# Whole-tile weight splits with three buffers a part, and woven weights prepared two pieces ahead

## The chip, the core and the metric

The program runs on one core of one Trainium2 chip. The metric is the device time of the whole program in microseconds. Three runs of the kernel before took 2589.87, 2593.4 and 2594.01 us; the median is 2593.4 us. The profile and the trace are of one further execution of the same kernel.

## The reference, cut to what matters

Two token groups (512 latent tokens and 128 context tokens, 640 columns in all) go through two layers. Everything is float32.

```python
def trunk_layer(x, cond, ...):
    mod = silu(cond) @ w_ada + b_ada            # six vectors of 1024 each
    h = rmsnorm(x) * (1 + scale1) + shift1
    q, k, v, z, a, b, u_ssm, u_pool, gates = split(h @ w_in)   # 1024 -> 6160 columns
    o_dn   = deltanet(q, k, v, z, a, b)         # chunked, two directions, 4 heads of 128
    o_ssm  = s5(u_ssm)                          # complex diagonal scan, two directions, then GLU
    o_pool = pool_mixer(u_pool)                 # windows 2, 4, 8, 16
    merged = g_dn * (o_dn @ w_branch_dn) + g_ssm * (o_ssm @ w_branch_ssm) \
           + g_pool * (o_pool @ w_branch_pool)
    x = x + gate1 * (merged @ w_out)
    h = rmsnorm(x) * (1 + scale2) + shift2
    return x + gate2 * (ffn(h))                 # 1024 -> 2 x 2816, conv3, silu gate, 2816 -> 1024
```

A final RMSNorm follows, and the last context states of both scans are outputs too.

## The kernel before, in words

**Products in three parts.** A float32 weight tile of 128 output columns arrives in SBUF as `wraw`, 128 partitions by 8 rows of 128 (1024 columns, 512 KB). `wsplit` (L362) makes two fp32r parts of it: `whi`, a rounded copy on ScalarE (called through the wrapper, so the trace gives it as L235 with output `whi`), and `wlo = wraw - whi` on VectorE (L372). `mm3` (L377) then runs, for each of the 8 rows, two matmuls of 320 columns with whi and the high part of the activations (L384), two with whi and the low part (L386) and two with wlo (L388): 48 matmuls a tile, in one double PSUM tile `acc`. In the trace these three lines are nearly all of TensorE's time.

**Buffers of the weights.** `wraw` has `WRAW` = 4 slots of 512 KB. The slots are shared by three users: the weight tiles, the tiles `wada` of w_ada (512 KB each; the adaLN vectors need two per k row, consumed by TensorE at L446 straight from the slot), and one small tile. A slot is given out in turn, so the n-th user waits for the release of the (n-4)-th. A weight tile's slot is released by its wlo; a wada slot by its matmuls. `whi` and `wlo` have `WB` = 4 buffers of `WK` = 4 rows each, so a tile takes two buffers of each part and is split by two ScalarE and two VectorE operations of 512 columns. All loads of weights are issued by SyncE (L359, L443), which also issues the other transfers of the layer and works them off in program order: a transfer that waits for its slot holds up the ones behind it.

**Weaving.** A layer has three long chains with little TensorE work: the S5 state-space stage (`s5_chain`: input products, `s5_in`, the scan on VectorE, `s5_out`), the DeltaNet stage, and the turn between layers. While such a chain is written out, `Weave.run` adds to a credit and emits pieces of other work from a queue `wv`: tiles of the input projection (z, pool, q, k, v, gates), branch products and the adaLN pieces. `Weave.step` emits one piece; where the piece that is next in the queue has weights, its weights are loaded and split ahead of it (`self.w`). What is left in the queue at a stage's end is drained without a chain beside it. The order of the instructions on each engine is then chosen by a list scheduler over the whole program; the code order and the buffers decide what it may choose from.

**S5 output.** For each of 8 groups `qd`, `s5_kernel` (L954) makes a table with matmuls at L964, finishes a small tile on VectorE (L970, L971), stores it to DRAM (L974) and reads it back in eight transfers (L979) as the Toeplitz tile `M`; `s5_out` (L982) multiplies the scanned states by the table (L997, L998) and the inputs by `M` (L999).

**FFN.** The FFN of layer 0 carries two adaLN groups of layer 1: after each weight tile comes one k row with two wada tiles. The FFN has no weave; its tiles are loaded and split one or two ahead by its own loop.

The names of rows in the trace: `whi`, `wlo`, `wraw`, `wada` as above; `pg` a page of the activation arena (its sizes are `PAGES`), `acc` and `sm` PSUM tiles, `hall_dram` and `s_hall` the small S5 tile.

Of the kernel before, what the change touches and what calls it, by code (L numbers as in the profile page):

```python
# [12 lines left out]
F32R = mybir.dt.float32r  # L13
AF = mybir.ActivationFunctionType
OP = mybir.AluOpType
AX = mybir.AxisListType

P = 128
D = 1024
KT = 8  # L20
# [14 lines left out]
NSLOT = 82  # L35
UNIT = 4
PAGE = 2592 // UNIT
PAGES = [5888] + [2592] * 2 + [2560] * 4 + [1280] * 11 + [2592]
EPS = 1e-6
WRAW = 4  # L40
WK, WB = 4, 4
OFF_Q, OFF_K, OFF_V, OFF_Z, OFF_AB = 0, 512, 1024, 1536, 2048
OFF_SSM, OFF_POOL, OFF_G = 2064, 2576, 3088
POOL_WINDOWS = (2, 4, 8, 16)
# [144 lines left out]
class Weave:  # L189
# [3 lines left out]
    def __init__(self, arena):  # L193
        self.arena = arena
        self.q = deque()
        self.credit, self.scale = 0.0, 1.0
        self.w = None

    def add(self, cost, fn, weights=None):

# [8 lines left out]
    def step(self):  # L209
        cost, fn, weights = self.q.popleft()  # L210
        self.arena.side = True
        w = [self.w or weights()] if weights else []
        self.w = self.q[0][2]() if self.q and self.q[0][2] else None
        fn(*w)
        self.arena.side = False
        self.credit -= cost
# [43 lines left out]
def hybrid_dit_kernel(ctx: ExitStack, tc: tile.TileContext, a, outs, depth=DEPTH, taps=None):  # L260
    nc = tc.nc
    V, S, GP, PE = nc.vector, ScalarE(nc.scalar), nc.gpsimd, nc.tensor

    cpool = ctx.enter_context(tc.tile_pool(name="cpool", bufs=1))
    wpool = ctx.enter_context(tc.tile_pool(name="wpool", bufs=1))
# [30 lines left out]

    ar = Arena(ctx.enter_context(tc.tile_pool(name="apool", bufs=1)), PAGES)

# [57 lines left out]
    def wraw(src, c0, nk, ncols):  # L356

        t = wpool.tile([P, nk, ncols], F32, name="wraw", tag="wraw", bufs=WRAW, padded_shape=[P, 8, P])
        nc.sync.dma_start(t, src.rearrange("(k p) m -> p k m", p=P)[:, :, c0:c0 + ncols])  # L359
        return t  # L360

    def wsplit(raw, m):  # L362

        his, los = [], []
        for k in range(0, raw.shape[1], WK):
            ks = slice(k, min(k + WK, raw.shape[1]))
            n = ks.stop - k
            hi = wpool.tile([P, n, P], F32R, name="whi", tag="whi", bufs=WB, padded_shape=[P, WK, P])
            lo = wpool.tile([P, n, P], F32R, name="wlo", tag="wlo", bufs=WB, padded_shape=[P, WK, P])
            src = raw[:, ks, m * P:(m + 1) * P]  # L370
            S.activation(hi, src, AF.Copy)
            V.tensor_sub(lo, src, hi)  # L372
            his.append(hi)
            los.append(lo)
        return Blocks(his), Blocks(los)

    def mm3(ps, w, hs, first=True, last=True, M=P):  # L377

        hi, lo = w
        n = hi.n  # L380
        for k in range(n):
            hh, hl = hs[k]
            for h in range(2):
                PE.matmul(ps[:M, h, :HF], hi[:, k, :M], hh[:, h * HF:(h + 1) * HF], start=first and k == 0, stop=False)  # L384
            for h in range(2):
                PE.matmul(ps[:M, h, :HF], hi[:, k, :M], hl[:, h * HF:(h + 1) * HF], start=False, stop=False)  # L386
            for h in range(2):
                PE.matmul(ps[:M, h, :HF], lo[:, k, :M], hh[:, h * HF:(h + 1) * HF], start=False,  # L388
                          stop=last and k == n - 1)
# [32 lines left out]
    class Stream:  # L422


        def __init__(self, src, c0, ncols, nk=KT):
            self.src, self.c0, self.nk = src, c0, nk

        def tile(self, m):
            return wsplit(wraw(self.src, self.c0 + m * P, self.nk, P), 0)


    def ada_pieces(l, p, mod, grp, E=None):
# [3 lines left out]
        def rows_k(k):  # L436
# [3 lines left out]
            for hf in range(2):  # L440
                t = E() if E else wpool.tile([P, 1024], F32, name="wada", tag="wraw", bufs=WRAW)
                c0 = grp * 2048 + hf * 1024
# [1699 lines left out]
```

## Time and profile before

| | before |
|---|---|
| runs shown | 2589.87, 2593.4, 2594.01 us |
| profiled execution, device time | 2591.93 us |
| its span in the trace | 2590.2 us |
| mean granted TensorE clock | 0.973 of full |
| TensorE matmul busy | 2440.7 us, 94% |
| VectorE busy | 1608.3 us, 62% |
| ScalarE busy | 989.8 us, 38% |
| GpSimd busy | 555.2 us, 21% |
| splits on ScalarE (whi) | 538 instructions, 331.7 us |
| splits on VectorE (wlo) | 538 instructions, 414.5 us |

The span is the time between the first and the last instruction of the profiled execution; the 1.7 us between it and the device time lie around it. The granted clock is the share of TensorE's full speed that the chip gave; 0.5 in a stretch is the lower of its two levels (1.2 and 2.4 GHz). Matmul records in the trace are pipelined, so a stretch where TensorE is busy all the time is read by how many matmuls it holds.

### The profile page before, as it was taken

How to read it: one execution, taken by the hardware profiler on the slowest of the kernel's cores; microseconds unless marked ns; L12 is line 12 of the kernel's file. 1: busy time of each engine (PE TensorE's matmuls, PEld its weight loads, DVE VectorE, ACT ScalarE, POOL GpSimd, SP SyncE). 2: the span in 40 equal slices, each digit the busy share in tenths (PEclk: the TensorE clock that was granted, in tenths of full speed). 3: DMA queues.
4: the chain of work that ended last, by engine and by line, in shares of the span. 5: the costliest groups of instructions: out<-in, count | busy, mean ns of one | idle time of the engine just before them, and what ended most of it. 6: DMA issues, size and time to landing. Idle time of an engine off the chain costs nothing. (4 is left out here: it accounts for less than half of the span.)

```text
span 2590.2 us, 43654 instructions
## 1 busy us (share of the span) xinstructions
PE 2440.7 (94%) x17225; PEld 2321.6 (90%) x17225; DVE 1608.3 (62%) x3250; ACT 989.8 (38%) x1792; POOL 555.2 (21%) x560
## 2 busy tenths in 40 slices
PE   7899989998889999999988999899989999999999
PEld 6688987997789988999988998799879899999998
DVE  5768863269866743553596687633897766445355
ACT  4242342363333531442443423424533354334243
POOL 3521320135342100000134404311445320000000
PEclk8899999999889999999999999999999999999999
DMA  9833327344253255322237232463454322222221
GB/s 309 162 112 94 91 64 233 114 127 140 94 178 95 74 172 178 98 67 81 75 115 103 59 113 79 118 197 99 138 166 160 112 66 74 74 74 78 78 66 66
DMA packets 382016, 297.29 MB, mean 115 GB/s; under 512 B 33706, under 2 KB 336500, under 8 KB 381812
## 3 DMA queue, kind: packets, MB, share of 16 engines
q1 hardware_dynamic: 377892, 286.53, 38.4%
q0 software_dynamic: 3552, 7.73, 1.2%
q8 instruction: 136, 2.23, 0.4%
q14 instruction: 68, 0.56, 0.1%
q10 hardware_dynamic: 368, 0.25, 0.0%
HBM read 251.45 MB, written 42.48 MB: 113 GB/s over the span
## 5 line engine op out<-in xcount | busy, mean ns | idle before, releaser
L384 PE MATMUL acc<-pg,whi 128*128 128x320 f32 x4064 | 943.2, 313 | 5.9 <-ACT pg L235 2.9
L388 PE MATMUL acc<-pg,wlo 128*128 128x320 f32 x4064 | 936.0, 311 | 8.0 <-DVE wlo L372 8.0
L386 PE MATMUL acc<-pg,whi 128*128 128x320 f32 x4064 | 938.0, 311 | 4.9 <-DVE pg L411 4.9
L372 DVE TENSOR_TENSOR wlo<-wraw,whi 128x512 fp32r<-128x512 f32 (+1 forms) x538 | 414.5, 776 | 524.3 <-ACT whi L235 518.1
L384 PEld LDWEIGHTS acc<-pg,whi 128*128 128x128 f32 x4064 | 681.4, 189 | 47.1 <-issue 16.7
L388 PEld LDWEIGHTS acc<-pg,wlo 128*128 128x128 f32 x4064 | 684.5, 189 | 10.5 <-DVE wlo L372 8.9
L386 PEld LDWEIGHTS acc<-pg,whi 128*128 128x128 f32 x4064 | 685.4, 189 | 6.0 <-DVE pg L411 5.4
L235 ACT ACTIVATE whi<-wraw 128x512 fp32r<-128x512 f32 (+1 forms) x538 | 331.7, 623 | 925.4 <-PE acc L386 723.0
L235 ACT ACTIVATE pg<-pg 128x640 f32<-128x640 f32 (+8 forms) x335 | 222.0, 682 | 262.5 <-DVE pg L1996 56.1
L235 ACT ACTIVATE pg<-sm 128x512 f32<-128x512 f32 (+9 forms) x245 | 109.5, 470 | 207.1 <-PE sm L1502 59.4
L235 ACT ACTIVATE pg<-acc 128x640 f32<-128x640 f32 (+3 forms) x196 | 127.0, 655 | 73.9 <-PE acc L388 49.5
L700 DVE SCALAR_TENSOR_TENSOR pg<-pg,cols_f 128x511 f32<-128x511 f32 (+1 forms) x130 | 65.9, 548 | 49.8 <-ACT pg L235 49.7
L411 DVE TENSOR_TENSOR pg<-pg,pg 128x640 fp32r<-128x640 f32 x84 | 68.6, 821 | 41.4 <-ACT pg L235 37.6
L713 POOL DMA_DIRECT2D pg<-in_ssm_lambda_re_dram x2 | 1.2, 583 | 407.9 <-ACT whi L235 407.9
L1685 POOL TENSOR_TENSOR pg<-pg,pg 128x640 f32<-128x640 f32 x21 | 38.9, 1855 | 226.1 <-DVE pg L1683 146.9
L691 DVE SCALAR_TENSOR_TENSOR pg<-acc,mod,pg 128x320 f32<-128x320 f32 x56 | 30.8, 549 | 78.3 <-PE acc L388 78.2
L235 ACT ACTIVATE pg<-acc,cols_f 128x640 f32<-128x640 f32 (+1 forms) x88 | 68.3, 776 | 0.0
L701 DVE SCALAR_TENSOR_TENSOR pg<-pg,cols_h 128x511 f32<-128x511 f32 (+1 forms) x130 | 65.6, 546 | 0.0
L446 PE MATMUL sm<-wada,silu_c 128*32 128x512 f32 x320 | 57.9, 627 | 8.0 <-DMA wada<-in_w_ada_dram 8.0
L1683 DVE SCALAR_TENSOR_TENSOR pg<-pg,acc 128x640 f32<-128x640 f32 x48 | 39.0, 817 | 40.9 <-PE acc L388 35.3
L906 POOL TENSOR_TENSOR pg<-pg,pg 128x512 f32<-128x512 f32 (+1 forms) x32 | 54.7, 1710 | 1.9
L901 POOL TENSOR_TENSOR pg<-s_cp,pg 128x640 f32<-128x640 f32 x16 | 27.6, 1725 | 127.4 <-PE acc L388 55.8
(392 smaller groups left out, 2960.8 us busy)
## 6 DMA issues: line engine op xcount, KB each, us to landing
wraw<-in_w_in_dram SPq DMA_DIRECT2D x96, 512.0 KB, 4.4
wraw<-in_ffn_w_up_dram SPq DMA_DIRECT2D x88, 512.0 KB, 3.9
wada<-in_w_ada_dram SPq DMA_DIRECT2D x80, 512.0 KB, 4.4
wraw<-in_ffn_w_down_dram SPq DMA_DIRECT2D x32, 512.0 KB, 3.9
mg_dram<-pg SPq DMA_DIRECT2D x32, 320.0 KB, 2.2
pg<-mg_dram SPq DMA_DIRECT2D x32, 320.0 KB, 5.2
wraw<-in_w_out_dram SPq DMA_DIRECT2D x16, 512.0 KB, 3.9
pg<-in_w_ada_dram SPq DMA_DIRECT2D x6, 1024.0 KB, 10.8
```

The costliest lines, as they stand in the source:

```text
L235: ins = self.engine.activation(out, in_, func, **kw)
L372: V.tensor_sub(lo, src, hi)
L384: PE.matmul(ps[:M, h, :HF], hi[:, k, :M], hh[:, h * HF:(h + 1) * HF], start=first and k == 0, stop=False)
L386: PE.matmul(ps[:M, h, :HF], hi[:, k, :M], hl[:, h * HF:(h + 1) * HF], start=False, stop=False)
L388: PE.matmul(ps[:M, h, :HF], lo[:, k, :M], hh[:, h * HF:(h + 1) * HF], start=False, stop=last and k == n - 1)
L411: V.tensor_sub(lo.r, src, hi.r)
L446: PE.matmul(ps[q:q + 32, :], silu_c[:, k, :], t[:, j * 512:(j + 1) * 512], start=k == 0, stop=k == KT - 1, tile_position=(0, q))
L700: V.scalar_tensor_tensor(y[:, b + 1:e], r[:, b:e - 1], w0, y[:, b + 1:e], op0=OP.mult, op1=OP.add)
L701: V.scalar_tensor_tensor(y[:, b:e - 1], r[:, b + 1:e], w2, y[:, b:e - 1], op0=OP.mult, op1=OP.add)
L906: E.tensor_tensor(oo, oo, t.f, op=OP.add if r else OP.subtract)
L1683: V.scalar_tensor_tensor(hv(g_.f), hv(g_.f), 1.0, ps[:, :, :HF], op0=OP.add, op1=OP.mult)
L1685: GP.tensor_tensor(g_.f, g_.f, mg.f, op=OP.add)
```

## The change

The split of a weight tile becomes one ScalarE and one VectorE operation over its 1024 columns (`WK` = 8); whi and wlo have three buffers of a full tile each (`WB` = 3; before, four half ones). The raw slots go from four to three. The first arena page gives up 128 columns. `Weave.step` keeps the weights of the next two pieces that have any, wherever they stand in the queue; before, it prepared those of the very next piece, and only if that piece had weights. The helper `wdma` and the flag `dma` are added, but nothing sets the flag.

```diff
-PAGES = [5888] + [2592] * 2 + [2560] * 4 + [1280] * 11 + [2592]
+PAGES = [5760] + [2592] * 2 + [2560] * 4 + [1280] * 11 + [2592]
 EPS = 1e-6
-WRAW = 4
-WK, WB = 4, 4
+WRAW = 3
+WK, WB = 8, 3
@@ class Weave
-        self.w = None
+        self.w = deque()
@@ def step(self):
         cost, fn, weights = self.q.popleft()
         self.arena.side = True
-        w = [self.w or weights()] if weights else []
-        self.w = self.q[0][2]() if self.q and self.q[0][2] else None
+        if weights and not self.w:
+            self.w.append(weights())
+        w = [self.w.popleft()] if weights else []
+        later = [x for _, _, x in self.q if x][:2]
+        while len(self.w) < len(later):
+            self.w.append(later[len(self.w)]())
         fn(*w)
@@ new helper, and its only caller
+    def wdma(src, c0, nk):
+        v = src.rearrange("(k p) m -> p k m", p=P)[:, :, c0:c0 + P]
+        hi = wpool.tile([P, nk, P], F32R, name="whi", tag="whi", bufs=WB, padded_shape=[P, WK, P])
+        lo = wpool.tile([P, nk, P], F32R, name="wlo", tag="wlo", bufs=WB, padded_shape=[P, WK, P])
+        GP.dma_start(hi, v)
+        S.activation(lo, hi, AF.Copy, scale=-1.0)
+        GP.dma_start(lo, v, accum_op=OP.add)
+        return Blocks([hi]), Blocks([lo])
@@ class Stream
-        def __init__(self, src, c0, ncols, nk=KT):
-            self.src, self.c0, self.nk = src, c0, nk
+        def __init__(self, src, c0, ncols, nk=KT, dma=False):
+            self.src, self.c0, self.nk, self.dma = src, c0, nk, dma
         def tile(self, m):
+            if self.dma:
+                return wdma(self.src, self.c0 + m * P, self.nk)
             return wsplit(wraw(self.src, self.c0 + m * P, self.nk, P), 0)
```

In the program, splits go from 538 to 297 on each of the two engines: 522 of 512 columns and 16 of 256 become 225 of 1024, 16 of 768 and 56 of 512 (the tiles of 4 rows). The numbers of TensorE, SyncE and GpSimd instructions stay. Line numbers of the new kernel are higher: L372 is L376, L359 is L363, L384, L386 and L388 are L399, L401 and L403, and lines from L443 on are higher by 17.

The order moves in the woven stages of both layers. Three places follow.

**VectorE in layer 0, while the tables of `s5_in` are made** (`s5_bp` and L900 to L906 are those tables, `acc_1124` and `acc_1112` the accumulator of the same z tile). Before:

```order
L900 TENSOR_TENSOR pg17_19_176<-s5_bp_773,pg6_12_130 128x512
L906 TENSOR_TENSOR pg18_13_132<-pg18_13_132,pg1_7_98 128x512
L1674 SCALAR_TENSOR_TENSOR pg7_29_1173<-pg7_29_1173,acc_1124 128x640
L906 TENSOR_TENSOR pg14_16_138<-pg14_16_138,pg5_11_126 128x512
L901 TENSOR_TENSOR pg18_13_132<-s5_bp_773,pg6_12_130 128x512
L906 TENSOR_TENSOR pg15_17_140<-pg15_17_140,pg5_11_126 128x512
L372 TENSOR_TENSOR wlo_1333<-wraw_1330,whi_1332 128x512
L372 TENSOR_TENSOR wlo_1337<-wraw_1330,whi_1336 128x512
```

The new kernel at the same place (L917, L918 and L923 are the table lines there):

```order
L917 TENSOR_TENSOR pg17_19_176<-s5_bp_761,pg6_12_130 128x512
L1691 SCALAR_TENSOR_TENSOR pg7_29_1161<-pg7_29_1161,acc_1112 128x640
L923 TENSOR_TENSOR pg18_13_132<-pg18_13_132,pg1_7_98 128x512
L923 TENSOR_TENSOR pg14_16_138<-pg14_16_138,pg5_11_126 128x512
L376 TENSOR_TENSOR wlo_1109<-wraw_1106,whi_1108 128x1024
L918 TENSOR_TENSOR pg18_13_132<-s5_bp_761,pg6_12_130 128x512
L923 TENSOR_TENSOR pg15_17_140<-pg15_17_140,pg5_11_126 128x512
```

The split of the tile now stands two table operations earlier. It belongs to the tile after next: the weights of the tile that TensorE takes up first after the z tile (`wlo_928`) are split 33 rows earlier, ahead of all the tables.

**TensorE in layer 0, between the second and the third group of `s5_out`** (`sm_2878` and `sm_2812` are the second group's output, `sm_3030` and `sm_2960` the third's; the L964 rows, L981 in the new kernel, make a later group's table). Before:

```order
L997 MATMUL sm_2878<-pg12_14_134,pg18_13_132 81x128
L998 MATMUL sm_2878<-pg12_14_134,pg18_13_132 81x128
L999 MATMUL sm_2878<-pg1_7_98,pg2_8_116 81x128
L964 MATMUL sm_2898<-pg13_15_136,pg6_12_130 32x128 x8
L964 MATMUL sm_2899<-pg13_15_136,pg6_12_130 32x128 x8
L997 MATMUL sm_3030<-pg17_19_176,pg18_13_132 81x128
L998 MATMUL sm_3030<-pg17_19_176,pg18_13_132 81x128
L999 MATMUL sm_3030<-pg1_7_98,pg2_8_116 81x128
```

The new kernel, from the last rows of the woven tile that now stands there:

```order
L399 MATMUL acc_3326<-pg4_27_519,whi_3062 128x320 x2
L401 MATMUL acc_3326<-pg4_27_519,whi_3062 128x320 x2
L403 MATMUL acc_3326<-pg4_27_519,wlo_3063 128x320 x2
L399 MATMUL acc_3410<-pg16_20_289,whi_3184 128x320
L981 MATMUL sm_2832<-pg11_28_1071,pg6_12_130 32x128 x8
L981 MATMUL sm_2833<-pg11_28_1071,pg6_12_130 32x128 x8
L1014 MATMUL sm_2960<-pg1_7_98,pg18_13_132 81x128
```

All 48 matmuls of the tile `acc_3326` and one of the next tile have come between the second group and the rows after it; before, none stood there.

**TensorE in layer 1, where the first adaLN tiles of the last group are used** (`sm_15995` and `sm_15401` are the accumulators of that group). Before:

```order
L1012 MATMUL sm_15882<-cst_72,pg3_95_12547 128x81 x4
L446 MATMUL sm_15995<-wada_15996,silu_c_107 32x512 x2
L446 MATMUL sm_15995<-wada_16000,silu_c_107 32x512 x2
L446 MATMUL sm_15995<-wada_16036,silu_c_107 32x512 x2
L446 MATMUL sm_15995<-wada_16040,silu_c_107 32x512 x2
L446 MATMUL sm_15995<-wada_16076,silu_c_107 32x512 x2
L446 MATMUL sm_15995<-wada_16080,silu_c_107 32x512 x2
L384 MATMUL acc_15963<-pg8_113_15946,whi_15959 128x320 x2
```

The new kernel, from the first pair of the same group on:

```order
L1029 MATMUL sm_15284<-cst_72,pg10_94_12665 128x81 x4
L463 MATMUL sm_15401<-wada_15402,silu_c_107 32x512 x2
L463 MATMUL sm_15401<-wada_15406,silu_c_107 32x512 x2
L399 MATMUL acc_15375<-pg3_103_15352,whi_15359 128x320 x2
L399 MATMUL acc_15416<-pg3_103_15352,whi_15365 128x320 x2
L401 MATMUL acc_15375<-pg3_103_15352,whi_15359 128x320 x2
L403 MATMUL acc_15375<-pg3_103_15352,wlo_15360 128x320 x2
```

Six wada tiles stood in a row; now one pair stands alone, 24 matmuls follow, then the second pair (8 rows below the last shown). The later wada tiles stand singly, 7 to 47 matmuls apart.

In the FFN of layer 0 the order is the same in both kernels: on SyncE two wada loads, then one weight tile, over and over, and on TensorE one pair of wada tiles, then the 48 matmuls of the weight tile that was loaded behind that pair.

## Rows read from the trace of the kernel before

**Rows 1.** The page: busy time by engine, and granted clock by slice

```profile
PE 2440.7 (94%) x17225; PEld 2321.6 (90%) x17225; DVE 1608.3 (62%) x3250; ACT 989.8 (38%) x1792; POOL 555.2 (21%) x560
PEclk8899999999889999999999999999999999999999
```

**Rows 2.** Windows: start:end, length, busy time by engine (instructions), granted clock, DMA share, GB/s

```profile
95.00:125.00 30.00, 17.62 (x86) 12.55 (x85) 29.96 (x25) 3.60 (x6) 27.58 (x22) 0.77 0.73 191
292.00:382.00 90.00, 77.48 (x721) 73.58 (x721) 59.63 (x89) 39.22 (x70) 37.17 (x41) 0.94 0.24 62
585.00:755.00 170.00, 143.10 (x1084) 134.97 (x1085) 138.20 (x277) 59.44 (x145) 79.07 (x68) 0.89 0.43 138
900.00:1300.00 400.00, 400.00 (x2728) 384.50 (x2727) 195.13 (x360) 143.13 (x225) 7.03 (x10) 1.00 0.38 111
1500.00:1700.00 200.00, 188.68 (x1469) 175.56 (x1468) 143.23 (x370) 71.94 (x123) 47.49 (x49) 0.97 0.40 119
```

**Rows 3.** Waits of TensorE: waiter <- releaser, us in total, times, longest

```profile
PE acc L388 <- DVE wlo L372: 8.0, 1, 8.0
PE sm L999 <- DMA hall_dram<-s_hall: 8.0, 1, 8.0
PE sm L446 <- DMA wada<-in_w_ada_dram: 8.0, 3, 3.9
PE acc L384 <- ACT whi L235: 0.4, 1, 0.4
```

**Rows 4.** Groups by form: splits of 512 columns, and operations of 1024

```profile
L372 DVE TENSOR_TENSOR wlo<-wraw,whi 128x512 fp32r<-128x512 f32 x522 | 407.8, 787 | 514.4 <-ACT whi L235 508.2 <-PE acc L388 5.6
L235 ACT ACTIVATE whi<-wraw 128x512 fp32r<-128x512 f32 x522 | 325.0, 630 | 906.7 <-PE acc L386 704.4 <-DMA wraw<-in_w_in_dram 49.4 <-issue 45.7
L546 DVE TENSOR_TENSOR pg<-wraw,pg 128x1024 fp32r<-128x1024 f32 x6 | 7.5, 1258 | 8.5 <-ACT pg L235 8.4
L235 ACT ACTIVATE pg<-wraw 128x1024 fp32r<-128x1024 f32 x7 | 7.4, 1061 | 8.8 <-DMA wraw<-in_ffn_w_up_dram 7.2 <-DMA wraw<-in_w_in_dram 1.5
```

**Rows 5.** Timeline of TensorE around the first place (idle before in brackets)

```profile
102.94 3.26 PE L446 MATMUL sm<-wada,silu_c 128*32 128x512 f32 x8 [3.90 <-DMA wada<-in_w_ada_dram]
117.91 0.90 PE L388 MATMUL acc<-pg,wlo 128*128 128x320 f32 x2 [8.04 <-DVE wlo L372]
```

**Rows 6.** Timeline of VectorE around the first place

```profile
112.94 1.75 DVE L901 TENSOR_TENSOR pg<-s_bp,pg 128x512 f32<-128x512 f32 x1
114.61 1.75 DVE L906 TENSOR_TENSOR pg<-pg,pg 128x512 f32<-128x512 f32 x1
116.28 3.27 DVE L372 TENSOR_TENSOR wlo<-wraw,whi 128x512 fp32r<-128x512 f32 x2
```

**Rows 7.** Timeline of TensorE around the second place

```profile
322.43 0.38 PE L998 MATMUL sm<-pg,pg 128*81 128x128 f32 x2
330.84 0.69 PE L999 MATMUL sm<-pg,pg 128*81 128x128 f32 x2 [8.04 <-DMA hall_dram<-s_hall]
```

**Rows 8.** Timeline of SyncE around the second place

```profile
317.50 0.39 SPq L359 DMA_DIRECT2D wraw<-in_ssm_glu_w_dram  x1
323.58 0.34 SPq L974 DMA_DIRECT2D hall_dram<-s_hall  x1
325.35 3.59 SPq L979 DMA_DIRECT2D pg<-hall_dram  x8
```

**Rows 9.** Timeline of TensorE around the third place

```profile
1669.45 1.92 PE L446 MATMUL sm<-wada,silu_c 128*32 128x512 f32 x4 [3.83 <-DMA wada<-in_w_ada_dram]
```

**Rows 10.** Timeline of SyncE in the FFN of layer 0

```profile
950.67 0.33 SPq L443 DMA_DIRECT2D wada<-in_w_ada_dram  x1
951.10 1.00 SPq L359 DMA_DIRECT2D wraw<-in_ffn_w_up_dram  x2
```

**Rows 11.** Timeline of ScalarE in the FFN of layer 0

```profile
958.28 1.15 ACT L235 ACTIVATE whi<-wraw 128x512 fp32r<-128x512 f32 x2 [0.54 <-DMA wraw<-in_ffn_w_up_dram]
```

**Rows 12.** Timeline of TensorE in the FFN of layer 0

```profile
950.01 1.06 PE L446 MATMUL sm<-wada,silu_c 128*32 128x512 f32 x8
958.25 1.06 PE L446 MATMUL sm<-wada,silu_c 128*32 128x512 f32 x8
```

## The prediction

> **What bounds the kernel now.** I read the page's busy times first, then the windows by stage, then TensorE's waits, then the timelines around the longest of them. The first row shows TensorE busy for 94% of the span and no other engine above 62%; the clock row shows which slices lost speed [rows 1]. So TensorE is the bound, and time can come only from its idle time (2590.2 - 2440.7 = 149.5 us) and from stretches at the lower clock (1 - 0.973 of the span, 70 us).
>
> Where these lie is read from the windows [rows 2]. From 900 to 1300 us, in the FFN, TensorE is busy all the time at full clock: 2728 matmuls in 400 us, 0.147 us each. Nothing that is done to the splits makes that faster. Idle time lies in the woven stages: 12.4 of 30 us around 110 us, 12.5 of 90 us in the S5 output of layer 0, 26.9 of 170 us in its DeltaNet stage, 11.3 of 200 us in the S5 stage of layer 1. Lost speed is one minus the clock, times the length: 6.9, 5.4, 18.7 and 6.0 us there.
>
> The waits say what these gaps end with [rows 3]: one wait of 8.0 us for a split (wlo), one of 8.0 us for the small S5 tile, three for adaLN weights (8.0 us), and 0.4 us for whi. In hundreds of tiles TensorE waited for a split twice.
>
> **The change part by part.** All terms are made against the profiled run: 2590.2 us of span, 1.7 around it, 2591.9 us; the median of the runs is 1.5 us above, inside their spread of 4 us.
>
> *Larger splits.* A tile costs ScalarE 2 x 630 ns before and 1061 ns after, by the copies of 1024 columns; VectorE 2 x 787 before and 1258 after [rows 4]. For 225 tiles that is 225 x 0.199 = 45 us less on ScalarE and 225 x 0.316 = 71 us less on VectorE (the 787 hold slow ones beside GpSimd, so 71 is the upper end). Both engines wait for buffers most of the time: whi 704 us for TensorE to free one, wlo 508 us for whi. By itself I put this at 0 for the end.
>
> *The first place, layer 0 at 110 us.* TensorE stands 8.04 us until 117.91 for a wlo that VectorE starts at 116.28, behind two table operations of 1.75 us [rows 5, 6]. In the new order this split stands two table operations earlier, so it starts at about 112.9, and as one operation it ends between 114.4 (1.26 us, rows 4) and 116.2 (the pair here took 3.27). And TensorE has 45 matmuls (6.6 us) of a tile that was split long before, with three adaLN tiles between them, so it arrives near 113. The gap shrinks to about 2.5 us: 5.5 saved, and 1 for the wait of 3.90 us ahead of it. Against it, the three slots let adaLN tiles load only as others leave; I expect two new waits of that kind within 40 us, 1.5 us together. Net -5; bounds -12 (both gaps go) and +5 (both stay, and the new waits are as long as the 3.9 seen).
>
> *The second place, S5 output of layer 0.* TensorE stands 8.04 us until 330.84 for the read-back of the small tile [rows 7]. Its path was: store at 323.58, read from 325.35 on, landed 330.8; a weight load sits in SyncE's queue ahead [rows 8]. Nothing in this path gets shorter, but 49 woven matmuls now stand ahead of the waiting one, 49 x 0.147 = 7.2 us of work. The work was to be done anyway, after the stage, so the end moves by what is filled. That removes 7 us of idle time and most of the 5.4 us of low clock that follows: -11. What is late next is the table after it, whose matmuls now stand 7 us later and whose read-back takes as long again; I give back 2. Net -9; bounds -17 (idle 12.5 and clock 5.4 nearly all gone) and 0 (the wait moves to the next group whole).
>
> *The third place, adaLN in layer 1.* Six wada tiles in a row met four slots: the fifth came after a wait of 3.83 us [rows 9], with some 3 us of low clock behind it (half of the 6.0 us of the window). Now 24 matmuls (3.5 us) stand after the first pair, and the first loads are issued earlier. Net -7; bounds -15 (with the smaller gaps of this window) and +3 (three slots make each single tile wait a little).
>
> *Three raw slots in the FFN of layer 0.* Here TensorE is fully busy, so a new wait is a loss. Fifteen periods of 8.24 us (950.01 to 958.25) hold two adaLN tiles and one weight tile each [rows 12]. With four slots one of the two adaLN tiles is loaded a period ahead. With three, both are issued only when the pair before has been used, and SyncE issues the weight tile behind them. The trace has three loads in a row, at 950.67, 951.10 and about 951.6, and ScalarE takes up the third at 958.28 [rows 10, 11], 8.27 us after the pair's start at 950.01. Then whi takes 1.06 and wlo 1.26: ready at +10.6. TensorE needs it at 8.24 + 1.06 + 4 x 0.147 = +9.9 (four matmuls with whi come first). So it is short by 0.7 us; as a late tile also delays the next pair, the shortfall is shared by two periods: 0.35 x 15 = +5. Bounds: 0 (the third load arrives 0.7 sooner) and +16 (it arrives 1.5 later: 1.1 x 15).
> At this place the trace shows halves: ScalarE's row holds two operations in 1.15 us, so the first half of whi is ready 0.43 us sooner than a whole one, and the first wlo half some 0.5 us sooner again [rows 4, 11]. The Trainium skill, in Perfetto Trace Analysis, Optimizing Scalar/DVE Operations, says that where these engines are not saturated but hold others up, breaking instructions up may let work finish sooner; the same section allows larger operations if the engine is saturated. By that rule the change goes the wrong way here, and with half operations this term would be about 0. The rows agree with it at this place alone; elsewhere the splits are done long before they are used.
>
> *DeltaNet stages, start, turn.* The 26.9 us of idle time at 585 to 755 [rows 2] lie in a chain of VectorE and TensorE with 138 of 170 us of VectorE; the filler for it is fixed (twelve tiles are kept back), so its gaps change places: 0, bounds -6 and +6. The first weight load is now issued behind the stores of x: +2, bounds 0 and +4. The smaller arena page and the unused helper: 0, since neither adds an instruction.
>
> *The sum.* -5 - 9 - 7 + 5 + 0 + 2 = -14: 2591.9 - 14 = 2578 us.
>
> **The rivals.**
> *The waits change places (2589 us).* The stages end with their chains, and woven work only moves the gaps. For it: the second place's path is a DMA round trip, and the next group's table now starts 7 us later. Against it: what is left of the woven work is drained at the end without a chain, so a filled gap stays saved. The sum: -5 at the first place, -1 at the second, -4 at the third (the idle, without the clock), +5 in the FFN, +2 elsewhere: -3.
> *Three slots throttle the loads (2609 us, slower).* One mechanism: adaLN tiles and weights share three slots in turn behind one queue, so the third load of each round comes too late. It decides from the point where that load is taken up later than 0.7 us before the 8.27 found here, and costs +16 in the FFN at 1.5 us later than found, +3 at the third place, +5 at the first; the second place keeps its -9, +2 elsewhere: +17. For it: the three loads row is from four slots, and new low-clock stretches could follow each gap. Against it: there are never more than three loads in flight, while 8.27 was found with other transfers near.
> *Whole splits come late wherever a tile is met fresh (2598 us).* 0.9 us (1061 - 630 and 1258 - 787 ns, rows 4) for each tile that TensorE reaches just as it is split. If a quarter of some 89 woven tiles were so, 20 us: 2578 + 20. Against it: two waits for splits in the whole trace, and pieces prepared two ahead. The section of the Trainium skill named above would have it so.
> *The change does not do what it says (2592 us).* The scheduler could undo the earlier preparation, and what is left are shorter operations off the bound. The order's three places speak against it.
>
> **How the numbers follow.** The forecast, 2578, has a chance of 0.60, with its own range of 2566 to 2589 from the terms' bounds, of which not all fall on one side. Changed places: 0.20. Throttled: 0.14. Whole splits late: 0.02. No effect: 0.04. A measurement here tells apart about 0.2%, 5 us: faster is below 2588. Faster takes the forecast but for its edge (0.57) and some of the second case (0.05): 0.62. Within: the rest of it, no effect, and the edges: 0.21. Slower: 0.17. The range runs from 2554, where the first three places give most of their lower bounds, to 2604, which takes in the no-change cases and half of the throttled one.
>
> **What would show it.** Right: no wait of L388's successor (L403) for wlo near 118 us above 4 us; the wait of L999's successor (L1016) for `hall_dram` under 3 us; no wait for wada near the end of layer 1's S5 stage above 2 us; ScalarE about 45 us and VectorE up to 71 us less busy. In the FFN of layer 0, waits of TensorE for wlo below 1 us each, and periods near 8.6 us. Wrong: periods of 9 us or more there, new waits for wada above 3 us in the S5 stages, or a wait of 7 us for the small tile one group later.

## The result and the profile after

The changed kernel takes 2625.7 us (median of four runs, 2620.2 to 2632.8) against 2593.7: a ratio of 1.0128, interval 1.0099 to 1.0157. It is slower by 32 us; 2578 was forecast, and 2604 was the upper end of the range. Its profiled execution took 2622.3 us, with a span of 2620.5.

The page shows the same matmuls, with less work on VectorE and ScalarE (rows to compare: [rows 1]):

```profile
PE 2453.1 (94%) x17225; PEld 2320.5 (89%) x17225; DVE 1566.5 (60%) x3009; ACT 951.8 (36%) x1551; POOL 543.8 (21%) x560
PEclk9998999998999999999989999999989999999999
```

VectorE has 42 us less work and ScalarE 38. Of the splits alone, ScalarE has 45 us less (331.7 to 286.3) and VectorE 42 (414.5 to 372.7): the larger operations did what was said of them. The groups by form show the cost of one [rows 4]:

```profile
L376 DVE TENSOR_TENSOR wlo<-wraw,whi 128x1024 fp32r<-128x1024 f32 x225 | 302.3, 1346 | 439.4 <-ACT whi L239 427.0 <-DMA V_dram<-pg 11.8 <-PE acc L403 0.3
L239 ACT ACTIVATE whi<-wraw 128x1024 fp32r<-128x1024 f32 x225 | 237.9, 1058 | 585.3 <-PE acc L401 427.1 <-DMA wraw<-in_w_in_dram 69.5 <-DMA wraw<-in_ffn_w_down_dram 51.7
```

Of the waits of TensorE that the prediction named, those for a split and for the small tile are gone or short. Those for adaLN weights are now five of 8.7 us together, where they were three of 8.0 [rows 3]:

```profile
PE sm L1431 <- ACT pg L239: 21.3, 3, 13.1
...
PE sm L463 <- DMA wada<-in_w_ada_dram: 8.7, 5, 4.2
...
PE acc L403 <- DVE wlo L376: 3.1, 8, 0.4
PE acc L399 <- ACT whi L239: 2.6, 6, 0.8
...
PE sm L1016 <- DMA hall_dram<-s_hall: 1.5, 1, 1.5
```

The wait of 8.0 us for wlo is now 0.4 at most, and the one for the small tile 1.5. But the first of these rows has grown: L1431 (L1414 before) waits 21 us for a copy. Before, the row was this, with all three waits in layer 0:

```profile
PE sm L1414 <- ACT pg L235: 7.5, 3, 3.3
```

After, 19.2 of the 21.3 us lie in the chunk chain of layer 1's DeltaNet stage, a place for which the prediction has no term.

Windows over the first four stages of [rows 2] (moved along with the stages, the fourth longer by 40 us) say the same:

```profile
95.00:125.00 30.00, 25.80 (x145) 19.20 (x144) 29.93 (x23) 4.39 (x7) 28.32 (x22) 0.94 0.68 190
280.00:370.00 90.00, 81.47 (x747) 77.13 (x747) 58.62 (x79) 36.34 (x62) 40.80 (x41) 0.96 0.26 69
575.00:740.00 165.00, 141.00 (x1108) 135.40 (x1109) 137.36 (x271) 57.72 (x139) 74.35 (x67) 0.92 0.42 134
850.00:1290.00 440.00, 434.28 (x2935) 413.90 (x2934) 205.81 (x335) 150.29 (x193) 5.88 (x8) 1.00 0.36 106
```

The first stretch has 145 matmuls where 86 were, at a clock of 0.94 instead of 0.77. The FFN (fourth row), which had no idle time, now has 5.7 us of it.

To find the loss, I cut the span at four instructions that both kernels issue, and took the length of each part (us, one profiled execution of each kernel; the line numbers are those of before). The cut at L519 stands ahead of the FFN; its last use in layer 0 lies inside the turn.

| part | before | after | difference |
|---|---|---|---|
| start to the first matmul of L519 (layer 0) | 830.0 | 814.6 | -15.4 |
| to the last L519 of layer 0 (FFN, most of the turn) | 509.1 | 520.2 | +11.1 |
| to the first L1363 of layer 1 (S5 stage, drained work) | 510.8 | 515.4 | +4.6 |
| to the first L1414 of layer 1 (DeltaNet, chunk chain) | 10.6 | 36.3 | +25.7 |
| to the end | 729.7 | 734.0 | +4.3 |

One stretch of 10.6 us holds 26 of the 30 us. What that is worth is seen in windows over layer 1's DeltaNet chain. Before, cut at 1849, 1860, 1960 and 2017 us:

```profile
1849.00:1860.00 11.00, 11.00 (x84) 10.94 (x83) 9.92 (x18) 4.46 (x12) 4.04 (x3) 1.00 0.34 128
1860.00:1960.00 100.00, 85.90 (x654) 81.58 (x653) 94.41 (x190) 37.47 (x89) 43.22 (x37) 0.98 0.41 132
1960.00:2017.00 57.00, 53.00 (x487) 50.04 (x487) 41.36 (x94) 22.03 (x55) 35.30 (x31) 1.00 0.61 207
```

After, the same parts of the chain, cut at 1850, 1886, 1986 and 2048 us:

```profile
1850.00:1886.00 36.00, 30.46 (x216) 30.20 (x214) 21.89 (x23) 11.59 (x17) 23.52 (x24) 0.98 0.60 205
1886.00:1986.00 100.00, 75.74 (x525) 70.37 (x526) 86.81 (x183) 34.66 (x83) 33.58 (x29) 0.83 0.26 83
1986.00:2048.00 62.00, 52.47 (x469) 50.22 (x468) 40.89 (x89) 18.83 (x51) 30.42 (x27) 0.92 0.56 185
```

The matmuls are as many: 1225 before (84 + 654 + 487), 1210 after. The chain starts late, the woven matmuls run on in the meantime (216 where 84 were), and they are missing later: idle time of TensorE grows from 18.1 to 39.3 us, and the clock of the middle 100 us falls from 0.98 to 0.83. The longest of the gaps stands there:

```profile
1943.33 2.13 PE L1431 MATMUL sm<-pg,cst 128*128 128x360 f32 x3 [13.13 <-ACT pg L239]
```

### The profile page after: what moved, and what is told of

Its sections match the earlier page's. It is cut to its first block, busy times and chain, and to the rows that moved or that the text cites. A ratio compares the mean times of both kernels' runs of the same rounds, so it can differ in the third digit from the quotient of the medians.

```text
span 2620.5 us, 42879 instructions
## 1 busy us (share of the span) xinstructions
PE 2453.1 (94%) x17225; PEld 2320.5 (89%) x17225; DVE 1566.5 (60%) x3009; ACT 951.8 (36%) x1551; POOL 543.8 (21%) x560
## 4 chain that ended last, share of the span: by engine, by line
PE 71%; DVE 13%; DMA 6%; ACT 3%; issue 2%; SPq 1%; POOL 1%; ACTq 0%; DVEq 0%; POOLq 0%
PE acc L399 19%; PE acc L401 19%; PE acc L403 19%; ACT pg L239 2%; DVE wlo L376 2%; PE sm L463 1%; DMA wraw<-in_w_in_dram 1%; PE sm L536 1%; DMA wraw<-in_ffn_w_down_dram 1%; DMA wraw<-in_ffn_w_up_dram 1%; ACT whi L239 1%; PE sm L940 1%; DVE pg L1404 1%; PE acc L420 1%; DVE pg L1484 1%
## 5 line engine op out<-in xcount | busy, mean ns | idle before, releaser
L399 PE MATMUL acc<-pg,whi 128*128 128x320 f32 x4064 | 945.1, 313 | 12.0 <-ACT pg L239 6.1
L401 PE MATMUL acc<-pg,whi 128*128 128x320 f32 x4064 | 940.5, 311 | 4.8 <-DVE pg L426 4.8
L403 PE MATMUL acc<-pg,wlo 128*128 128x320 f32 x4064 | 939.2, 311 | 3.1 <-DVE wlo L376 3.1
L399 PEld LDWEIGHTS acc<-pg,whi 128*128 128x128 f32 x4064 | 683.0, 189 | 47.1 <-ACT pg L239 13.7
L401 PEld LDWEIGHTS acc<-pg,whi 128*128 128x128 f32 x4064 | 685.9, 189 | 15.8 <-issue 8.6
L403 PEld LDWEIGHTS acc<-pg,wlo 128*128 128x128 f32 x4064 | 684.9, 189 | 15.4 <-issue 8.7
L376 DVE TENSOR_TENSOR wlo<-wraw,whi 128x1024 fp32r<-128x1024 f32 (+2 forms) x297 | 372.7, 1257 | 525.3 <-ACT whi L239 510.8
L239 ACT ACTIVATE whi<-wraw 128x1024 fp32r<-128x1024 f32 (+2 forms) x297 | 286.3, 966 | 802.5 <-PE acc L401 601.2
L239 ACT ACTIVATE pg<-pg 128x640 fp32r<-128x640 f32 (+8 forms) x335 | 222.4, 684 | 441.2 <-DVE pg L718 121.3
L463 PE MATMUL sm<-wada,silu_c 128*32 128x512 f32 x320 | 64.5, 605 | 8.7 <-DMA wada<-in_w_ada_dram 8.7
L1702 POOL TENSOR_TENSOR pg<-pg 128x640 f32<-128x640 f32 x16 | 31.5, 1969 | 163.9 <-DVE pg L1700 120.1
L717 DVE SCALAR_TENSOR_TENSOR pg<-pg,cols_f 128x511 f32<-128x511 f32 x98 | 49.5, 548 | 23.4 <-ACT pg L239 21.4
L586 POOL TENSOR_SCALAR pg<-pg,ada_a 128x320 f32<-128x320 f32 (+2 forms) x27 | 26.5, 990 | 133.5 <-DVE pg L708 61.7
L420 PE MATMUL acc<-pg,pg 128*128 128x320 f32 x144 | 38.1, 345 | 16.6 <-DVE pg L598 14.4
L1702 POOL TENSOR_TENSOR pg<-pg,pg 128x640 f32<-128x640 f32 x16 | 33.4, 2089 | 96.1 <-DVE pg L1700 94.7
```

Of the source, the lines that this page charges most:

```text
L239: ins = self.engine.activation(out, in_, func, **kw)
L420: PE.matmul(ps[:, :HF], x[:, k, :], y[:, h * HF:(h + 1) * HF], start=first and n == 0, stop=last and n == 2)
L463: PE.matmul(ps[q:q + 32, :], silu_c[:, k, :], t[:, j * 512:(j + 1) * 512], start=k == 0, stop=k == KT - 1, tile_position=(0, q))
L717: V.scalar_tensor_tensor(y[:, b + 1:e], r[:, b:e - 1], w0, y[:, b + 1:e], op0=OP.mult, op1=OP.add)
L1702: GP.tensor_tensor(g_.f, g_.f, mg.f, op=OP.add)
```

## The experiments

### The change's own parts: preparation, operation size, depth in one stage

The first theory for this jump was that pieces prepared two ahead put splits ahead of the chain on ScalarE and VectorE. The rivals were the three slots and the whole operations.

**e1_one_ahead** gives the changed kernel the old rule:

```diff
-        later = [x for _, _, x in self.q if x][:2]
-        while len(self.w) < len(later):
-            self.w.append(later[len(self.w)]())
+        if not self.w and self.q and self.q[0][2]:
+            self.w.append(self.q[0][2]())
```

> The new kernel with the old weave rule (weights of the very next queue entry only); whole-tile splits, three buffers a part and three raw slots stay. Theory 1, splits prepared two pieces ahead stand ahead of the DeltaNet chain of layer 1 on VectorE and ScalarE: the jump of 26 us in layer 1's DeltaNet stage goes, and so do most of the gains of layer 0; the FFN keeps its 4 to 5 us; 2592 to 2602 us. Rival, three raw slots: the jump stays, 2612 to 2626. Rival, whole splits come late: the jump stays, 2612 to 2626.

Measured: 2635.7 us, ratio 1.0164 (1.0148 to 1.0181), above both ranges that were set down, and 10 us slower than the changed kernel (whose interval this one touches). The late stretch stays, at 34.1 us. So two ahead is not the cause; that it is a gain is seen more clearly in e8 and e9 below.

**e2_half_ops** goes back to half operations:

```diff
-WK, WB = 8, 3
+WK, WB = 4, 6
```

> The new kernel with splits in half operations of 512 columns again and six half buffers a part (the same memory); two ahead and three raw slots stay. Theory 1: the splits stand in the same places, so the jump in layer 1's DeltaNet stage stays at 15 us or more; 2612 to 2630 us. Rival, whole splits come late: the jump goes, 2585 to 2600. By the three slots: as the new kernel, and the FFN's 4 to 5 us shrink to under 2, since the first halves are ready about 0.9 us sooner.

Measured: 2625.3 us, 1.0123 (1.0102 to 1.0144), the stretch 37.8 us. Whole operations are not the cause either. The FFN's loss, which was to shrink under 2 us, grew: its stage in layer 0 takes 487.1 us, against 473.2 before.

**e3_dn1_depth1** keeps two ahead up to layer 1's DeltaNet queue and one from there on:

```diff
+        wv.depth = 1 if l else 2
```

> The new kernel with one weighted piece prepared ahead instead of two in layer 1 from the DeltaNet stage on; all else as in the new kernel. Theory 1: the jump of 26 us there shrinks below 8, the stages before it keep their times; 2596 to 2608 us. Rivals, three raw slots or whole splits: the jump stays, 2616 to 2628.

Measured: 2621.2 us, 1.0107 (1.0081 to 1.0133), the stretch 36.2 us. The theory of the splits fell with this.

**e5_whole_only** is the kernel before with whole operations (two buffers a part, so the same memory):

```diff
-WK, WB = 4, 4
+WK, WB = 8, 2
```

> The kernel before with whole-tile splits alone: two full buffers a part (the same memory), four raw slots, old weave rule. Theory 1: within 8 us of before, 2588 to 2602, for two full buffers release later than four halves, and a tile is ready later by up to 0.9 us. Rival, whole splits come late: 2612 or more, with new waits for splits in many places.

Measured: 2603.4 us, 1.0036 (1.0019 to 1.0054): 11 us slower by itself, just above the range that was set down. The stretch is 13.7 us, so the jump is not here. With two full buffers instead of four halves the kernel also gets its buffers back in larger pieces; the run does not tell that from the size of the operations. The part with the FFN and the turn is 6.5 us longer, what comes after it 7.2 together.

### The arena page

What e1, e2 and e3 have in common are the three raw slots and the first arena page, of 5760 columns instead of 5888. (Three slots alone, e4 below, leave the stretch at its 10.6 us.) With 5888 the page has room beside the scan's X (5248 columns) for just one tile of 640; with 5760 such a tile goes to another page, and later allocations differ with it. The new theory: no instruction is added, but a tile gets a page that comes free later.

**e7_pages_only** is the kernel before with that constant alone:

```diff
-PAGES = [5888] + [2592] * 2 + [2560] * 4 + [1280] * 11 + [2592]
+PAGES = [5760] + [2592] * 2 + [2560] * 4 + [1280] * 11 + [2592]
```

> The kernel before with the first arena page at 5760 columns and nothing else changed. New theory, the smaller page: the jump of 20 us or more in layer 1's DeltaNet stage is there, 2610 to 2630 us. Rivals, three raw slots or the buffers: no jump, 2588 to 2600.

Measured: 2607.7 us, 1.0057 (1.0036 to 1.0078): 16 us slower. The stretch is 37.5 us, as expected. The total is below the range that was set down, since 8 us of the jump's 27 come back ahead of L519 (822.2 us, 830.0 before).

**e8_bigpage** is the changed kernel with the old page; the memory for it comes from a small buffer that two stages now share:

```diff
-PAGES = [5760] + ...
+PAGES = [5888] + ...
-        gr = small("dn_gr", P)
+        gr = small("s5_so", P)
```

> The new kernel with the first arena page at its old 5888 columns (the 512 bytes a partition come from two small tiles of different stages, s5_so and dn_gr, that now share one buffer). New theory, the smaller page: other pages are handed out, and GpSimd's preparation of the DeltaNet steps (L1551, L1552) comes ahead of the chunk chain's L1386 in layer 1, which costs the jump of 24 us in three kernels so far. Then the jump shrinks below 6 and the end is 2592 to 2604 us, or below before if the gains of layer 0 stay. Rival, three raw slots or three full buffers cause it: the jump stays, 2615 or more.

Measured: 2606.8 us, 1.0056 (1.0038 to 1.0073), 19 us faster than the changed kernel and 3 above the range that was set down; the stretch is 14.1 us. Page and stretch go together in both directions. (Sharing the buffer that the rates are stored from is a second edit; e7 above and e13 below do without it.)

The timelines of GpSimd say how. L1833 (L1850 after) loads the chunk chain's rates into arena tiles. Before:

```profile
1811.81 1.18 POOL L1833 DMA_DIRECT2D pg<-gr_dram  x2 [27.40 <-DVE pg L1631]
...
1815.43 2.04 POOL L1369 TENSOR_TENSOR pg<-pg,dn_tok 128x512 f32<-128x512 f32 x2 [1.38 <-DMA pg<-gr_dram]
```

After:

```profile
1838.59 0.62 POOL L1850 DMA_DIRECT2D pg<-gr_dram  x1 [48.06 <-DVE pg L1648]
1841.78 0.54 POOL L1850 DMA_DIRECT2D pg<-gr_dram  x1 [2.56 <-DVE pg L1638]
1842.34 1.04 POOL L1386 TENSOR_TENSOR pg<-pg,dn_tok 128x512 f32<-128x512 f32 x1
1845.51 1.59 POOL L1386 TENSOR_TENSOR pg<-pg,dn_tok 128x512 f32<-128x512 f32 x1 [2.13 <-DMA pg<-gr_dram]
1847.05 0.55 POOL L1850 DMA_DIRECT2D pg<-gr_dram  x1
```

The releaser in brackets is not the data but the destination's page (`pg`): its last reader on VectorE. The first load starts at 1838.6 instead of 1811.8, and the first operation on what it brings (L1369, L1386 after) at 1842.3 instead of 1815.4. It is not the same load: in the order of the program before, GpSimd's first two loads are those of chunk 0, with which the chain starts; in the changed kernel they are those of chunks 2 and 1, and chunk 0's is the third, at 1847.05, 35 us later than before. The programs name the pages too. The layer's first four loads go to pages 5, 1, 3 and 3 in the kernel before and in e8, and to pages 15, 10, 3 and 3 in e7 and in the changed kernel. The same row in e8 and the same wait in e7:

```profile
1826.56 1.18 POOL L1850 DMA_DIRECT2D pg<-gr_dram  x2 [28.45 <-DVE pg L1648]
```

```profile
POOL pg L1833 <- DVE pg L1631: 46.7, 1, 46.7
```

27.4 and 28.5 us with the large page, 48.1 and 46.7 with the small one. All kernels that were run fall into these two groups, e13 below aside: the first load stands 33 to 39 us ahead of the first L1363 of layer 1 in the eight with the large page, and 11.6 to 11.7 us in the six with the small one.

One other reading was left: the stage's preparation (`dn_prep`) stands ahead of the chain on GpSimd and SyncE. **e11_prep_pinned** holds it behind the last chunk product, in the changed kernel (cut; the comment is added):

```diff
+        g, sd = st["marks"]        # last tensor_tensor and store of chunk 3
+        with after(g), after(sd):
+            dn_prep_(d, c, tk, st)
```

> The new kernel, small page and all, with the preparation of the DeltaNet steps (L1549 to L1552) held behind the last L1397 and L1398 of chunk 3 on GpSimd and on SyncE's queue. Theory, the small page costs time because that preparation lands in the free page 0 and is then issued ahead of the chunk chain: the stretch from the chunk's first L1365 group to the first L1414 of layer 1 falls from 36 us to 16 to 24, and the end to 2605 to 2615 us. Rival, other effects of the re-dealt pages (waits for stores of pages that are handed on) set the stretch: it stays above 30, 2618 or more.

Measured: 2620.3 us, 1.0111 (1.0086 to 1.0136); the stretch goes from 36.3 to 32.5 us only, and the wait stays:

```profile
1839.14 0.62 POOL L1857 DMA_DIRECT2D pg<-gr_dram  x1 [47.72 <-DVE pg L1655]
```

Both are what the rival of its expectation said. So the preparation is at most 4 of 26 us. **e13_rates_page0** leaves the page small and moves only the rates tiles, into page 0:

```diff
-                st["E", c] = ar.take(512), ar.take(512)
+                st["E", c] = ar.take(512, big=True), ar.take(512, big=True)
```

> The new kernel, small page and all, with the DeltaNet rates tiles (L1850's destinations) taken from page 0, which is free then. Theory, the small page hands the first rates tile a page that VectorE (L1648) releases some 20 us later than before: GpSimd's first wait there falls from 48 to about 27 us, the stretch from the chunk's first L1380 group to the first L1431 of layer 1 from 36 to 10 to 20 us, and the end to 2598 to 2610 us. Rival, several re-dealt pages each hold the chain up: the stretch stays above 28, 2614 or more.

Measured: 2604.5 us, 1.0050 (1.0026 to 1.0074), 21 us faster than the changed kernel. GpSimd, and TensorE at the first L1431:

```profile
1819.18 5.39 POOL L1850 DMA_DIRECT2D pg<-gr_dram  x10 [5.68 <-DMA gr_dram<-dn_gr]
```

```profile
1871.17 2.06 PE L1431 MATMUL sm<-pg,cst 128*128 128x240 f32 x11
```

The load now waits for its data, and the stretch is 13.8 us. The same row of the changed kernel had been this:

```profile
1886.51 1.92 PE L1431 MATMUL sm<-pg,cst 128*128 128x240 f32 x4 [6.05 <-ACT pg L239]
```

The cause of the jump is shown: the late page of the rates tiles. What the other re-dealt pages cost or give was not separated.

### What is left with the page mended

**e9_one_ahead_bigpage** is e8 with the old rule of preparation (the edits of e8 and e1 together).

> Whole-tile splits with three buffers a part, three raw slots, the old weave rule, and the first arena page at 5888 columns (as in the run with the big page). New theory: no jump in layer 1's DeltaNet stage; against the run with the small page and the old weave rule (2635.65) some 25 us less, 2605 to 2615, for the losses of that kernel in layer 0 stay if they are the slots'. Rival, the slots cause the jump: 2630 or more.

Measured: 2624.3 us, 1.0115 (1.0083 to 1.0146), above the 2605 to 2615 that were set down: with the old rule the page is worth 11 us (e1 against e9), not 25. Against e8, two ahead is worth 17 us, and layer 0 shows it: the part up to L519 is 837.4 us in e9, 821.0 in e8.

**e4_wraw3_only** is the kernel before with three raw slots:

```diff
-WRAW = 4
+WRAW = 3
```

> The kernel before with three raw slots and nothing else changed. New theory: no jump in layer 1's DeltaNet stage; the FFN of layer 0 loses 3 to 6 us with its adaLN tiles; 2594 to 2608 us. Rival, three raw slots throttle the loads: the jump is there, 2612 or more.

Measured: 2609.1 us, 1.0071 (1.0051 to 1.0090): 17.5 us slower, just above the range that was set down, and with no jump: the stretch is 10.6 us. In one profiled execution (some 8 us above the median) it is +6.1 up to L519, +12.7 in the FFN and the turn (all of it in the FFN, for which 3 to 6 had been set down), +4.3 in layer 1's S5 stage. TensorE in the FFN of layer 0, rows with idle time and the adaLN pairs that start a period:

```profile
931.63 1.06 PE L446 MATMUL sm<-wada,silu_c 128*32 128x512 f32 x8
933.03 0.56 PE L384 MATMUL acc<-pg,whi 128*128 128x320 f32 x2 [0.33 <-ACT whi L235]
...
940.40 1.06 PE L446 MATMUL sm<-wada,silu_c 128*32 128x512 f32 x8
942.25 0.56 PE L384 MATMUL acc<-pg,whi 128*128 128x320 f32 x2 [0.78 <-ACT whi L235]
...
949.63 1.06 PE L446 MATMUL sm<-wada,silu_c 128*32 128x512 f32 x8
```

Periods of 8.77 and 9.23 us instead of 8.24, each with a wait for whi.

**c3_half_bigpage** is e8 with half operations (`WK, WB = 4, 6`): two ahead, three slots.

> The new kernel with the big page (as in that run, 2606.84) and splits in half operations with six half buffers. Theory, the size of a split costs little where three tiles are buffered: 2598 to 2608 us, of it the FFN's 4 to 6 us with the three slots. Rival, whole splits come late: below 2595.

Measured: 2620.4 us, 1.0114 (1.0095 to 1.0133), 14 us slower than e8 and above both ranges that were set down. The FFN of layer 0 alone takes 488.1 us, and 479.7 in e8. With e4, e8 and e9 it makes four kernels with three slots and the large page (us; buffers a part in brackets):

| | old rule | two ahead |
|---|---|---|
| half operations | 2609.1 (e4, four half ones) | 2620.4 (c3, six half ones) |
| whole operations | 2624.3 (e9, three full ones) | 2606.8 (e8, three full ones) |

Neither part has a price of its own. Two ahead, with the buffers for a third tile, costs 11 us with half operations and saves 17 with whole ones; whole operations cost 15 with the old rule and save 14 with two ahead. Why, no run tested.

**c1_two_after and c2_one_weighted** keep everything of before but the rule. In c2 the weights of the next piece that has any are prepared before a piece is emitted, past pieces without weights (cut; the comment is not in the kernel):

```diff
-        w = [self.w or weights()] if weights else []
-        self.w = self.q[0][2]() if self.q and self.q[0][2] else None
+        w = [self.w.popleft() if self.w else weights()] if weights else []
+        self.ahead(1)        # fills self.w from the queue's pieces with weights
         fn(*w)
```

c1 adds `self.ahead(2)` behind `fn`.

> The kernel before (four raw slots, half splits in four half buffers, first page 5888) with a weave that keeps the next weighted piece prepared before a piece is written and the second one after it, so that no buffer more is needed. Theory, two ahead is worth 10 to 17 us and the loss is the smaller page's and the third slot's: 2574 to 2586 us, no jump in layer 1's DeltaNet stage, FFN periods of 8.24 us. Rival, the gain of two ahead needs the third full buffer: 2588 to 2598. Rival, two ahead is a loss wherever splits queue ahead of a chain: above 2600.

> The kernel before with one weighted piece prepared ahead, found past pieces without weights (before: only where the very next queue entry had weights). Theory: most of the gain of two ahead comes from not missing the pieces behind adaLN and pool pieces; 2578 to 2590 us. Rival, depth two is what counts: 2588 to 2598.

Measured: c1 2587.5 us, 0.9984 (0.9971 to 0.9997); c2 2586.3 us, 0.9972 (0.9961 to 0.9983). Both beat both kernels, c2 by 0.28% against before and inside the range that was set down; c1, at 0.16% with an interval that ends just below 1, missed the 2574 to 2586 that were set down. The two cannot be told apart, so preparing a second piece shows no gain here beyond finding the next one with weights. The part of c2 up to L519 is 822.2 us (830.0 before), and the rest keeps its lengths within 3 us. Four slots, half operations and the old page keep what the changed kernel lost.

## Why the prediction was wrong, by its steps

- **The three places were right.** The first: the wait for wlo is gone. The second: 8.0 us became 1.5. The third: 3.83 us became 0.19, in this row [rows 9]:

```profile
1678.94 1.05 PE L463 MATMUL sm<-wada,silu_c 128*32 128x512 f32 x4 [0.19 <-DMA wada<-in_w_ada_dram]
```

  The terms for layer 0 (-5, -9, 0 for its DeltaNet, +2) add up to -12; measured -15.4. That they come so near is partly luck: 6.4 of it is the page's (e8, with the old page, has -9.0). The wait of about 4 us ahead of the first place stayed (4.2), where I had credited 1 us, and the two new waits behind it took 1.2 and 1.7, where I had 1.5 for both. (The earliest end of the split there is 112.9 + 1.26 = 114.2, not 114.4; nothing hangs on it.) The third term, -7, cannot be seen: its part of the span is 4.6 us longer, for layer 1's S5 stage, which holds that place, takes 13 us more with the small page (below).
- **"The smaller arena page and the unused helper: 0, since neither adds an instruction" is the step that failed.** The helper indeed costs nothing. The page costs 16 us alone (e7), and 19 in the changed kernel (e8); 26 in its stretch. I costed instructions, where the page decides which buffer a tile gets and so when it may start. "Its gaps change places: 0, bounds -6 and +6" was for layer 0's DeltaNet stage, and layer 1's was not looked at. No rival covered it: of the four, none had a wait for a page.
- **The three slots: mechanism right, size of the FFN right, the rest too small.** The FFN stage of layer 0, taken by itself, went from 473.2 to 479.3 us: +6, with +5 forecast. TensorE of the changed kernel there [rows 12]:

```profile
912.39 1.06 PE L463 MATMUL sm<-wada,silu_c 128*32 128x512 f32 x8
920.95 1.06 PE L463 MATMUL sm<-wada,silu_c 128*32 128x512 f32 x8
922.35 0.56 PE L399 MATMUL acc<-pg,whi 128*128 128x320 f32 x2 [0.34 <-ACT whi L239]
923.61 0.56 PE L403 MATMUL acc<-pg,wlo 128*128 128x320 f32 x2 [0.41 <-DVE wlo L376]
930.26 1.06 PE L463 MATMUL sm<-wada,silu_c 128*32 128x512 f32 x8
```

  The tile is short by 0.34 us for whi and 0.41 for wlo, together the 0.7 that was worked out. Periods run from 8.23 to 9.79 us; 8.6 was expected, and the 9 us that was to speak against it occurred too. (The kernel before has eleven periods of 8.24 us in that stage, not fifteen.) The FFN's loss is not the same in every kernel with three slots: +6 to +15 us. But three slots alone cost 17.5 us over the whole program (e4). The mechanism of the throttling rival is real, and the forecast had it too low. That the rival's sum was +17 is luck: it holds -9 for the second place and +2, which e4 does not have, and its losses alone are 24. In the changed kernel four slots were never run, so what going from four to three costs there is not shown.
- **Larger operations at "0 for the end" depends on what stands around them.** Alone they cost 11 us (e5). In the changed kernel they cost nothing (e2, with halves, is as slow), and with the old page they save 14 (c3 against e8). In the FFN of e5 they cost nothing (472.5 us, 473.2 before). Part of e5's loss is in the turn, 55.6 us before and 59.7 in e5: there 332 matmuls stand in a window of 60 us, and 300 in one of 56 before; 32 x 0.147 = 4.7 us of work has moved in. Why the time is not won back later stays open.
- **The rule on breaking up.** At the FFN, where splits hold TensorE up and neither engine is saturated, I weighed half operations at about 0 us instead of +5. The runs show no such gain, rather the reverse: with three slots the FFN of layer 0 takes 479 to 483 us with whole operations in six kernels (after, e1, e3, e8, e9, e11) and 485.7 in a seventh (e13), and 486 to 488 with halves (e2, e4, c3), one profiled execution each. So the advice of the Trainium skill (Perfetto Trace Analysis, Optimizing Scalar/DVE Operations) is not borne out at this place. Why halves are not faster there was not settled.

Put together from runs in steps that follow each other: three slots and whole operations +33 (e9 against before), two ahead -17 (e8 against e9), the small page +19 (the changed kernel against e8) make +34; the change measured +32. The prices of single parts (+17.5, +11, -10 by e1, +16) add up to nearly the same, but that is luck, since they hold in other surroundings and the four kernels above show how far they can differ there. So the page's part is shown; how the rest divides between slots and operations in the changed kernel stays open. Open is also why layer 1's S5 stage itself lasts 252.6 us before and 263.8 to 266.2 in the six kernels with the small page, of which the drained work behind it gives back 9 to 15. With the large page it takes 250 to 255, and 259.2 in e13, so the page has a hand in it.

## What to carry to other kernels

A constant that sizes a buffer pool is a change of order: it decides which buffer a tile gets and whose last reader it waits for. When a change touches one, compare the destinations of every stage's first operations, and run that constant alone; it cost one line here and explained more than half the loss. An edit that adds no instruction has a cost with two ends like any other. And the price of a part holds where it was measured: two ahead saved 17 us beside whole operations and cost 11 beside halves.

## What the runs showed of the hardware

One split of VectorE in the late stretch of the changed kernel took 7.37 us where its neighbour took 1.22. VectorE:

```profile
1857.97 1.22 DVE L376 TENSOR_TENSOR wlo<-wraw,whi 128x1024 fp32r<-128x1024 f32 x1 [11.77 <-DMA V_dram<-pg]
1865.02 7.37 DVE L376 TENSOR_TENSOR wlo<-wraw,whi 128x1024 fp32r<-128x1024 f32 x1 [5.82 <-ACT whi L239]
1872.32 0.68 DVE L1389 SCALAR_TENSOR_TENSOR pg<-pg 128x512 f32<-128x512 f32 x1
```

GpSimd beside it, the first and last of six operations that follow each other without a gap:

```profile
1865.04 1.03 POOL L1552 TENSOR_TENSOR pg<-pg,dn_tok 128x512 f32<-128x512 f32 x1
...
1870.28 1.03 POOL L1386 TENSOR_TENSOR pg<-pg,dn_tok 128x512 f32<-128x512 f32 x1
```

The split ends at 1872.39, 1.08 us after the last of the six. In this trace all 188 splits of this form with no GpSimd operation beside them took 1.21 to 1.23 us, and every one that took longer (up to 8.78 us) had one beside it. The Trainium skill (SBUF — State Buffer, Who interferes with whom) says that an operation of VectorE with two SBUF inputs contends with one of GpSimd that reads SBUF, and that such contention is an exclusive lock. The rows agree with the exclusion; here the wait lasted through a whole row of six. No run took the GpSimd operations away.
